# Token gathers of 128 rows in place of 96 or 64 in a mixture-of-experts layer

## The chip, the core and the metric

The kernel is one program on one core of a Trainium2 chip. The metric is the device time of one execution in microseconds. Engines are named as the profile names them: PE is TensorE (PEld its weight loads), DVE VectorE, ACT ScalarE, POOL GpSimd, SP SyncE. SP and POOL also issue DMAs, each on a queue of its own, and both queues are served by the core's 16 DMA engines.

## The reference

One decoder layer on 512 tokens of width 1024, all in float32: two kinds of attention with one output projection, a layer norm giving x1, then a mixture of experts and a second layer norm. The part that matters here is the experts:

```python
logits = xf @ w_router + b_router            # 512 tokens, 32 experts
top_vals, top_idx = lax.top_k(logits, 4)
gates = softmax(top_vals)
...
g = minimum(xb @ w_gate[e] + b_gate[e], 7)   # xb: the tokens of expert e
u = clip(xb @ w_up[e] + b_up[e], -7, 7)
h = g * sigmoid(1.702 * g) * (u + 1)
y_rows = h @ w_down[e] + b_down[e]
...
y = sum over k of gates[n, k] * y_rows[dest[n, k]]
```

Each expert has three matrices of 1024 x 1024 in float32, 12.58 MB, so the 32 experts hold 402.7 MB. With 2048 assignments an expert has 64 tokens on average.

## The kernel before

**Stages.** Attention, first layer norm and routing come first; x1 is written to `x1d` in DRAM, a row of 4 KiB for each token. Then the experts run one after the other, a step each (`Step`, lines 1103 to 1158; the loop is at line 1631). The experts are ordered by their number of tokens and dealt out to the steps alternately: the 16 fullest are *large* steps with 96 slots (64 and 32 more), the others *small* steps with 64 slots. From step 1 to step 29 large and small alternate: 15 large, 14 small. The last two experts, the emptiest, are routed as a pair. Tokens that find no slot would go through a loop behind the end (`overflow`), which has nothing to do for these inputs.

**A step.** `gate0`/`gate1`, `up` and `down` multiply the step's tokens with the three matrices. 64 slots are done with 64 columns of the array twice beside each other (`mat64`, line 624), a large step's other 32 slots with 32 columns four times (`mat32`, line 634, `matd32`, line 1046). The result, scaled by the gates, is added to `accd` in DRAM by one or two accumulating indirect DMAs on POOL's queue (`store`, line 1157): 128 rows of 2 KB (two per slot), and in a large step 128 rows of 1 KB.

**Weights.** `wload` (line 662) brings each matrix in two DMAs of 2 MB, 128 partitions of 16 KiB, issued by SP into a ring of eight tiles and one further tile (`wtile`, line 655). A tile is free again when PE has read it for the last time, and SP waits for that before it issues.

**Tokens of a step.** Two steps ahead, `do_route` makes the token numbers: a product with a one-hot matrix (`route_mm`, line 969) gives for each slot the number of its token in `ix`; an unfilled slot gets 0. The one-hot matrix has 128 columns: for 64 slots these are slots 0 to 63 twice, for the other 32 (the second column of `ix`) slots 64 to 95 four times. So `ix` has 128 rows, and those past the slots repeat slots of the same expert. `gather` (line 975) casts the numbers to integers in `ii` on DVE (lines 977, 979) and issues one indirect DMA on POOL (line 981) that reads those rows of `x1d` into the tile `xg`, slot by slot on the partitions. There is one `xg` buffer. `load_x` (line 1031) transposes the 64 or 96 rows on PE (line 1039) and ACT copies them out (line 1040).

**Other gathers.** Step 0's is written out on its own at line 864 (64 rows). That of the last two experts is at line 1027 (`route_pair`): 64 slots of each, 128 rows in one DMA. Step 1's goes through `route_tokens` and `gather`, steps 2 to 29 through `route` and `gather`.

Of the kernel before, what the change touches and what calls it, by code (L numbers as in the profile page):

```python
# [19 lines left out]
P = 128  # L20
# [82 lines left out]
def kernel(ctx: ExitStack, tc: tile.TileContext, a: dict, out: bass.AP, dbg=None):  # L103
    nc = tc.nc
    dbg = dbg or {}
    V, S, G, PE = nc.vector, nc.scalar, nc.gpsimd, nc.tensor
# [9 lines left out]
    x1d = dr.tile([T, D], F32, name="x1d")  # L116
# [856 lines left out]
                          start=(t == 0), stop=(t == NT - 1))  # L973

    def gather(n, ii, ix, large):
        Cn = 96 if large else 64
        V.tensor_copy(ii[0:64], ix[0:64, 0:1])  # L977
        if large:
            V.tensor_copy(ii[64:96], ix[64:96, 1:2])
        xg = p3.tile([P, D], F32, tag="xg", name=f"xg{n}")  # L980
        G.indirect_dma_start(out=xg[0:Cn], out_offset=None, in_=x1d,  # L981
                             in_offset=bass.IndirectOffsetOnAxis(ap=ii[0:Cn], axis=0))
        return xg

    def route_info(n, oh, rhs_t, large):
# [9 lines left out]
    def route_tokens(n, oh):  # L995
        px = bank(f"pxt{n}")
        route_mm(px, oh, lambda t: RT[:, t, 0:2, n], True, 0, 2)
        xs, ix, gt, ii = route_tiles(n)
        V.tensor_copy(xs[:, :, 0:2], px[:, 0:16].rearrange("p (a b) -> p a b", a=2)[:, :, 0:2])
        V.tensor_tensor(ix, xs[:, :, 0], xs[:, :, 1], ALU.add)  # L1000
        return xs, gather(n, ii, ix, True), ix, gt
# [8 lines left out]
    def route(n, oh, rhs_t, large):  # L1010
        ii, ix, gt = route_info(n, oh, rhs_t, large)
        return gather(n, ii, ix, large), ix, gt
# [700 lines left out]
```

## Time and profile before

| | us |
|---|---|
| median of 3 runs | 1354.06 |
| lowest, highest | 1352.81, 1355.06 |
| the profiled execution | 1354.38 |
| its span | 1352.6 |
| PE busy in the span | 1240.9 (92%) |
| DVE, ACT, POOL busy | 392.3, 262.7, 179.0 |
| queue q1 (SP's): packets, MB | 34848, 428.15 |
| queue q0 (POOL's): packets, MB | 10880, 24.78 |

The span runs from the first to the last instruction of the program; the execution takes 1.8 us more. PE's busy time is that of pipelined matmuls with modelled ends. The DMA share is the mean share of time in which the 16 DMA engines had a packet in work, from each packet's own duration, so it can exceed 1; the GB/s are the bytes of those packets.

### The profile page before, as it was taken

How to read it: one execution, taken by the hardware profiler on the slowest of the kernel's cores; microseconds unless marked ns; L12 is line 12 of the kernel's file. 1: busy time of each engine (PE TensorE's matmuls, PEld its weight loads, DVE VectorE, ACT ScalarE, POOL GpSimd, SP SyncE). 2: the span in 40 equal slices, each digit the busy share in tenths (PEclk: the TensorE clock that was granted, in tenths of full speed). 3: DMA queues.
4: the chain of work that ended last, by engine and by line, in shares of the span. 5: the costliest groups of instructions: out<-in, count | busy, mean ns of one | idle time of the engine just before them, and what ended most of it. 6: DMA issues, size and time to landing. Idle time of an engine off the chain costs nothing.

```text
span 1352.6 us, 20619 instructions
## 1 busy us (share of the span) xinstructions
PE 1240.9 (92%) x8596; PEld 577.6 (43%) x8596; DVE 392.3 (29%) x1020; ACT 262.7 (19%) x588; POOL 179.0 (13%) x184
## 2 busy tenths in 40 slices
PE   9999998898999999898989898989797989899985
PEld 8887555443344343333333333333333333333331
DVE  6765667453121211111111111111111111111125
ACT  5544655231101111011101010101010101010113
POOL 0540221001011011011010101010101010100013
PEclk9999999898999999999999999999999999899978
DMA  8031064489999999999999999999999999999992
GB/s 312 0 125 63 7 256 171 172 333 358 380 390 401 394 381 403 395 401 394 403 396 402 394 399 399 398 398 400 397 398 396 402 394 401 397 420 409 420 377 97
DMA packets 45824, 454.28 MB, mean 336 GB/s; under 512 B 5856, under 2 KB 8672, under 8 KB 20256
## 3 DMA queue, kind: packets, MB, share of 16 engines
q1 hardware_dynamic: 34848, 428.15, 78.3%
q0 software_dynamic: 10880, 24.78, 7.4%
q8 instruction: 69, 1.13, 0.3%
q14 instruction: 27, 0.22, 0.0%
HBM read 436.39 MB, written 16.52 MB: 335 GB/s over the span
## 4 chain that ended last, share of the span: by engine, by line
PE 57%; DMA 38%; DVE 2%; issue 1%; ACT 0%; SPq 0%; POOL 0%; POOLq 0%; DVEq 0%; ACTq 0%
DMA wu<-w_up 33%; PE pu L624 10%; PE pg L624 9%; PE pd L624 9%; PE puz L634 3%; PE mx L556 3%; DMA wd<-w_down 3%; PE pd L1046 2%; PE pj L200 2%; PE pj L201 2%; PE pj L202 2%; PE pxg L1039 1%; DMA xg<-x1d,ii 1%; PE sc L469 1%; PE av L510 1%; PE pgz L634 1%
## 5 line engine op out<-in xcount | busy, mean ns | idle before, releaser
L624 PE MATMUL pd<-wd,hT 128*64 128x512 f32 x1024 | 231.2, 602 | 14.1 <-DMA wd<-w_down 14.1
L1157 POOL DMA_INDIRECT accd<-y,si x46 | 73.5, 1598 | 534.4 <-ACT y L1162 356.6
L624 PEld LDWEIGHTS pd<-wd,hT 128*64 128x64 f32 x1024 | 73.5, 138 | 158.2 <-issue 138.6
L624 PE MATMUL pg<-wg,xgB 128*64 128x512 f32 x512 | 123.4, 626 | 17.2 <-DMA wg<-w_gate 17.2
L624 PE MATMUL pu<-wu,xgB 128*64 128x512 f32 x512 | 118.9, 618 | 0.0
L624 PE MATMUL pg<-wg,xgA 128*64 128x512 f32 x512 | 117.9, 600 | 0.0
L624 PE MATMUL pu<-wu,xgA 128*64 128x512 f32 x512 | 114.6, 596 | 1.8 <-DMA wu<-w_up 1.8
L1062 DVE TENSOR_SCALAR u<-pu 128x512 f32<-128x512 f32 x31 | 21.4, 691 | 324.6 <-PE pu L628 324.5
L634 PE MATMUL puz<-wu,xgB 128*32 128x256 f32 x960 | 70.7, 447 | 46.2 <-DMA wu<-w_up 46.2
L624 PEld LDWEIGHTS pg<-wg,xgB 128*64 128x64 f32 x512 | 38.6, 142 | 88.9 <-issue 87.0
L981 POOL DMA_INDIRECT xg<-x1d,ii x29 | 27.3, 941 | 350.5 <-DVE ii L977 232.7
L634 PEld LDWEIGHTS puz<-wu,xgB 128*32 128x32 f32 x960 | 34.2, 124 | 85.6 <-DMA wu<-w_up 38.3
L1040 ACT COPY xgB<-pxg 128x384 f32<-128x384 f32 (+1 forms) x32 | 14.6, 472 | 286.0 <-PE pxg L1039 285.9
L624 PEld LDWEIGHTS pu<-wu,xgB 128*64 128x64 f32 x512 | 36.5, 143 | 75.1 <-issue 74.5
L624 PEld LDWEIGHTS pu<-wu,xgA 128*64 128x64 f32 x512 | 34.9, 137 | 73.1 <-issue 66.9
L624 PEld LDWEIGHTS pg<-wg,xgA 128*64 128x64 f32 x512 | 34.8, 137 | 61.1 <-issue 59.5
L1062 DVE TENSOR_SCALAR uz<-puz 128x256 f32<-128x256 f32 x16 | 6.8, 424 | 185.5 <-PE puz L638 185.5
L1046 PE MATMUL pd<-wd,hT 128*32 128x256 f32 x1024 | 58.8, 381 | 0.0
L634 PE MATMUL pgz<-wg,xgB 128*32 128x256 f32 x960 | 57.1, 391 | 0.0
L1162 ACT ACTIVATE y<-pd,gt 128x512 f32<-128x512 f32 x30 | 20.6, 687 | 170.3 <-PE pd L624 170.3
L1052 DVE TENSOR_SCALAR g<-pg 128x512 f32<-128x512 f32 x32 | 22.1, 691 | 89.0 <-PE pg L628 89.0
L1040 ACT COPY xgA<-pxg 128x256 f32<-128x256 f32 x30 | 11.2, 372 | 189.2 <-PE pxg L1039 188.2
(447 smaller groups left out, 1517.3 us busy)
## 6 DMA issues: line engine op xcount, KB each, us to landing
wg<-w_gate SPq DMA_DIRECT2D x64, 2048.0 KB, 40.0
wu<-w_up SPq DMA_DIRECT2D x64, 2048.0 KB, 40.0
wd<-w_down SPq DMA_DIRECT2D x62, 2048.0 KB, 40.1
wd<-w_down SPq DMA_DIRECT2D x3, 1024.0 KB, 33.0
hat<-wB SPq DMA_DIRECT2D x1, 2048.0 KB, 12.8
hwk<-wB SPq DMA_DIRECT2D x1, 2048.0 KB, 17.0
hwv<-wB SPq DMA_DIRECT2D x1, 2048.0 KB, 7.2
hwk<-w_o SPq DMA_DIRECT2D x1, 2048.0 KB, 7.3
```

The lines of the kernel that those rows point to most:

```text
L200: PE.matmul(o, xh[:, k, tt], h[:, 0:n], start=(k == 0), stop=False)
L201: PE.matmul(o, xh[:, k, tt], l[:, 0:n], start=False, stop=False)
L202: PE.matmul(o, xl[:, k, tt], h[:, 0:n], start=False, stop=(k == KD - 1))
L556: PE.matmul(ps[h], attnT[:, k, t * P:(t + 1) * P], wo[k // 4][:, k % 4, hs], start=(k == 0), stop=(k == KD - 1))
L624: PE.matmul(ps[64 * c:64 * c + 64, :], xt[:, k, 0:64], w[k // 4][:, k % 4, hf * 512:(hf + 1) * 512], start=(st and k == 0), stop=(k == KD ...
L634: PE.matmul(o[32 * c:32 * c + 32, :], xt[:, k, 64:96], w[k // 4][:, k % 4, c * 256:(c + 1) * 256], start=(k == 0), stop=False)
L981: G.indirect_dma_start(out=xg[0:Cn], out_offset=None, in_=x1d, in_offset=bass.IndirectOffsetOnAxis(ap=ii[0:Cn], axis=0))
L1040: S.copy(xgT[:, 4 * h:4 * h + 4, 0:Cn], pt[:, :, 0:Cn])
L1046: PE.matmul(ps[32 * c:32 * c + 32, 0:256], ht[:, k, :], wd[k // 4][:, k % 4, c * 256:(c + 1) * 256], start=(k == 0), stop=(k == KD - 1))
L1052: V.tensor_scalar(g, pgt, 7.0, None, ALU.min)
L1062: V.tensor_scalar(u, pup, 7.0, -7.0, ALU.min, ALU.max)
L1157: G.indirect_dma_start(out=dst, out_offset=bass.IndirectOffsetOnAxis(ap=si[:, i:i + 1], axis=0), in_=self.y[:, lo:hi], in_offset=None, com ...
```

## The change

`gather` casts all 128 rows of the token numbers and gathers 128 rows in every step. For a small step rows 64 to 127 are the slots 0 to 63 again; for a large step rows 64 to 127 are the slots 64 to 95 twice. Nothing else is changed: `load_x` reads the rows that it read.

```diff
     def gather(n, ii, ix, large):
-        Cn = 96 if large else 64
-        V.tensor_copy(ii[0:64], ix[0:64, 0:1])
         if large:
-            V.tensor_copy(ii[64:96], ix[64:96, 1:2])
+            V.tensor_copy(ii[0:64], ix[0:64, 0:1])
+            V.tensor_copy(ii[64:P], ix[64:P, 1:2])
+        else:
+            V.tensor_copy(ii, ix[:, 0:1])
         xg = p3.tile([P, D], F32, tag="xg", name=f"xg{n}")
-        G.indirect_dma_start(out=xg[0:Cn], out_offset=None, in_=x1d,
-                             in_offset=bass.IndirectOffsetOnAxis(ap=ii[0:Cn], axis=0))
+        G.indirect_dma_start(out=xg, out_offset=None, in_=x1d,
+                             in_offset=bass.IndirectOffsetOnAxis(ap=ii, axis=0))
         return xg
```

## Rows read from the trace of the kernel before

**Rows 1.** The page, the span in 40 slices: DMA share in tenths, GB/s.

```profile
DMA  8031064489999999999999999999999999999992
GB/s 312 0 125 63 7 256 171 172 333 358 380 390 401 394 381 403 395 401 394 403 396 402 394 399 399 398 398 400 397 398 396 402 394 401 397 420 409 420 377 97
```

**Rows 2.** The page, the chain that ended last: by engine, by line.

```profile
PE 57%; DMA 38%; DVE 2%; issue 1%; ACT 0%; SPq 0%; POOL 0%; POOLq 0%; DVEq 0%; ACTq 0%
DMA wu<-w_up 33%; PE pu L624 10%; PE pg L624 9%; PE pd L624 9%; PE puz L634 3%; PE mx L556 3%; DMA wd<-w_down 3%; PE pd L1046 2%; PE pj L200 2%; PE pj L201 2%; PE pj L202 2%; PE pxg L1039 1%; DMA xg<-x1d,ii 1%; PE sc L469 1%; PE av L510 1%; PE pgz L634 1%
```

**Rows 3.** The chain in order of time: start us, us, what.

```profile
366.46 7.02 PE pu L624 x32
...
423.75 7.02 PE pu L624 x32
...
581.65 7.85 PE pu L624 x32
...
607.56 37.84 DMA wu<-w_up
...
648.80 7.02 PE pu L624 x32
```

**Rows 4.** Windows: from:to, length, busy us by engine, PE clock, DMA share, GB/s.

```profile
320.00:345.00 25.00, 20.49 (x198) 9.20 (x198) 3.77 (x11) 1.79 (x4) 2.52 (x2) 0.86 0.92 318
345.00:366.00 21.00, 21.00 (x156) 8.77 (x155) 4.42 (x13) 3.06 (x6) 2.52 (x2) 1.00 0.99 401
...
716.76:1300.00 583.24, 527.89 (x3760) 211.42 (x3762) 94.34 (x256) 56.74 (x112) 58.18 (x46) 0.96 1.02 401
```

**Rows 5.** Windows, POOL alone: weights (2), gathers of 64, 96, 128, scatters (2).

```profile
592.00:599.00 7.00, 0.94 (x1) 1.00 1.01 430
...
1196.00:1203.00 7.00, 1.42 (x2) 1.00 1.00 428
414.60:421.60 7.00, 0.43 (x1) 1.00 0.99 342
...
1133.50:1140.50 7.00, 0.34 (x1) 1.00 1.01 346
561.50:568.50 7.00, 0.00 (x0) 1.00 1.03 344
...
1165.50:1172.50 7.00, 0.00 (x0) 1.00 1.02 337
1204.50:1211.50 7.00, 0.85 (x1) 1.00 1.02 428
611.00:618.00 7.00, 0.00 (x0) 1.00 1.04 386
555.50:561.50 6.00, 0.94 (x1) 1.00 1.03 394
```

**Rows 6.** Tile xg, whole span, then 590:610, 620:645 and 1195:1215: duration ns, start, landing.

```profile
L981 POOL DMA_INDIRECT xg<-x1d,ii x29: 923/942/959, 292.3 to 1161.7; - x29
...
L981 POOL DMA_INDIRECT xg<-x1d,ii x1: 942/942/942, 596.3 to 596.3; - x1
...
DMA to landing us min/median/max: 9.7/9.7/9.7
...
L1039 PE MATMUL pxg<-cst,xg x8: 270/271/318, 621.2 to 622.1; 64*128 64x64 f32 x8
...
L1027 POOL DMA_INDIRECT xg<-x1d,ii x1: 1019/1019/1019, 1200.5 to 1200.5; - x1
...
DMA to landing us min/median/max: 10.8/10.8/10.8
```

**Rows 7.** Step 2's gather (landing, PE's wait) and casts in order of time.

```profile
DMA to landing us min/median/max: 9.0/9.0/9.0
...
324.94 1.11 PE L1039 MATMUL pxg<-cst,xg 64*128 64x64 f32 x8 [4.51 <-DMA xg<-x1d,ii]
...
595.39 0.15 DVE L977 CAST ii<-ix 64x1 int32<-64x1 f32 x1
```

## The prediction

> **What bounds the kernel now.** I read the page's slices first. From the tenth slice to the last but one the DMA digit is 9 and the GB/s line stays between 358 and 420 [rows 1]. The chain of work that ended last is shared between TensorE and DMA, and nearly all its DMA is one entry, the wait for the up weights (33% of the span) [rows 2]. In order of time the chain changes character. Early on a pair of experts (one large step, one small step) follows from TensorE alone: the up projection at 366.46 and the next at 423.75 are 57.3 us apart. Later the same pair takes 581.65 to 648.80, which is 67.2 us, and it has a weight transfer of 37.84 us in it [rows 3]. So TensorE could run a pair in 57.3 us and the weight stream needs 67. Before 345 us the stream sometimes has no free ring slot (318 GB/s, DMA share 0.92 in 320 to 345). From 345 us on the share is about 1 up to 1300 us [rows 4]. In that long stretch the time is the work of the DMA engines, and a transfer on the GpSimd queue costs what it takes from the weights beside it.
>
> The DMA share cannot price that: it counts the time packets took, and reads about 1 whether packets are fast or stretched. GB/s can. Rows 5 give it for short stretches. With weights alone the core moves 430, 433 and 428 GB/s (three stretches, the first and last shown), mean 430.3. Around a 64-row gather, seven stretches of 7 us lie between 328 and 349 GB/s, mean 340.1 (first and last shown). Around a 96-row gather, six lie between 337 and 347, mean 343.0 (first and last shown). Around the only gather on 128 rows, that of line 1027 for the last two experts, the stretch reads 428 GB/s, like weights alone [rows 5]. That is the observation on which the forecast rests: the short gathers take away far more than their own bytes, and the 128-row one does not.
>
> **Price of one gather.** The price is the stretch, less the time the weights moved in it would have taken alone: 7 us - (7 us x GB/s - own bytes) / 430.3. A row is 4 KiB.
> - 64 rows (262 KB): 7 - (2381 - 262)/430.3 = 2.08 us.
> - 96 rows (393 KB): 7 - (2401 - 393)/430.3 = 2.33 us.
> - 128 rows (524 KB): 7 - (2996 - 524)/430.3 = 1.26 us.
>
> The prices can be checked on a whole pair. Its weights, 2 x 12.58 MB at 430.3, take 58.5 us. Two scatters of 128 x 2 KB (386 GB/s in 7 us, 1.33 us each) and one of 128 x 1 KB (394 GB/s in 6 us, 0.81 us) make 3.5 us [rows 5]. With gathers of 2.08 and 2.33 us the sum is 66.4 us, against the 67.2 seen [rows 3]. At the 128-row gather's price per row the two short gathers would make only 1.6 us, and the sum would be 3.6 us short of what is seen, so their excess is real work of the stream and not a local blur.
>
> **The change part by part.**
> - *Gathers in the saturated stretch.* Line 981 issues 29 gathers, from 292.3 us on [rows 6]. Those of steps 1 to 3 come before 345 us. The other 26 are 13 of 64 rows and 13 of 96, since large and small steps alternate. If each then costs what the one at line 1027 costs, a small one saves 2.08 - 1.26 = 0.82 us and a large one 2.33 - 1.26 = 1.07 us: 13 x 0.82 + 13 x 1.07 = 24.6 us. For the new gather I take line 1027's price because it has the same form: 128 rows of 4 KiB from x1d into the same tile, through one index column, in the same stream. The other end is the price per row of the short gathers (rivals). A better price than 1.26 us is hardly possible, since 524 KB alone are 1.22 us at 430.3 GB/s.
> - *The three early gathers.* Up to 345 us the weight stream is held by ring slots that TensorE has yet to free, so a cheaper gather there is given back: nothing gained. One of them costs. Step 2's gather lands 9.0 us after issue and TensorE stands 4.51 us for it [rows 7]. The 64-row gather at 596.3 landed after 9.7 us, the 128-row one after 10.8 [rows 6]. TensorE thus waits 1.1 to 1.8 us longer, frees its slots later by as much, and the stream idles for it. I take +1.5 us, with bounds 0 and 1.8.
> - *Landing later elsewhere.* The gather at 596.3 landed by 606.0, and its first reader, the transposes of line 1039, starts at 621.2 [rows 6]. That is 15 us of cover for 1 to 2 us. If the cover were gone TensorE would stand for the difference once a step, at most 26 x 1.8 us, but TensorE has 67.2 - 57.3 = 10 us to spare in each pair.
> - *Issue on GpSimd.* 1.02 us against 0.94 a gather [rows 6], +0.08 us 29 times. What is queued behind is the scatter of the step's result, which waits for TensorE anyway: 0.
> - *Index casts.* A small step still has one cast, on 128 rows instead of 64; a large one still two, the second on 64 rows instead of 32. A cast of 64 x 1 takes 0.15 us [rows 7]; between nothing and as much again, 0.15 us per gather, which the 15 us of cover hide: 0.
> - *Unchanged.* The load into TensorE still reads only 96 or 64 rows of the tile (line 1039), so there is no more work behind it. Line 864's early gather and the pair's at 1027 are not touched. The rows added hold repeats that nobody reads.
>
> Sum: -24.6 + 1.5 = -23.1 us. The profiled execution took 1354.4 us (span 1352.6), so 1331.3. The median of the runs shown is 0.3 us below that execution. Forecast **1331 us**.
>
> [...]
>
> **Rivals.**
> 1. *Bytes only (slower).* Line 1027's gather is a single sample, and it may be cheap for its place, late in the stream, not for its 128 rows. Then added rows cost what its rows cost, 1.26/128 = 9.8 ns each: +0.63 us per small and +0.31 us per large gather, 13 x 0.94 = +12.3, with the early wait +13.8 us: **1368 us**. For it: one sample. Against it: weights alone move 428 GB/s just before it and 430 at 592 us [rows 5], so the stream is not easier there. [...]
> 2. *Price per row of the short gathers (slower).* If the cause is the gather's rows as such, a small one adds 64 x 2.08/64 = 2.08 us and a large one 32 x 2.33/96 = 0.78 us: 13 x 2.86 = +37, with the wait **1393 us**. Against it: line 1027 again, and that 96 rows cost only 1.12 times 64. The point from which it turns: a 128-row gather above 2.15 us, that is under 373 GB/s in its 7 us, makes the kernel slower.
> 3. *Half the gain.* The added rows read the same rows of x1d as slots of the other half, at about the same moment, and this may cost. Unfilled slots already all read token 0, at line 1027 too, and nothing shows there. **1343 us.**
> 4. *Nothing moves.* The stream gets faster and another bound takes over. TensorE's 57.3 us against some 65.3 for the new pair [rows 3] leaves no room for it; only a stream that runs dry after 345 us could do it. Within 0.2% (2.7 us, about what a measurement of this kernel can tell from no change): **1354 us**.
>
> **How the numbers follow.** Forecast 0.77, rival 3 0.08, rival 4 0.04, rival 1 0.07, rival 2 0.04. The forecast's own range is 1325 to 1338: the early wait at 0 and a GB/s reading off by 2 or 3 in each stretch on one side, 0.7 of the gain on the other. To 1345 it takes in rival 3, and 0.85 of the chance. Faster by over 0.2%: 0.77 + 0.08 = 0.85; same 0.04; slower 0.07 + 0.04 = 0.11.
>
> **What the changed profile would show.** Right: 7 us stretches around gathers after 345 us at about 425 GB/s instead of 340; pairs of about 65.3 us; bytes on the software queue up by 5.6 MB (1376 rows) and the span shorter all the same; TensorE's wait for step 2's gather near 6 us instead of 4.5. Wrong: gathers' stretches still near 340 to 370 GB/s (rivals 1 and 2), stretches at 425 but pairs still at 67 (rival 4), or stretches around 385 (rival 3). The forecast as a whole falls if line 1027's gather is cheap for another reason than its 128 rows.

## The result and the profile after

The changed kernel takes 1334.73 us (median of 4 runs, 1332.74 to 1337.12) against 1354.56 us for the kernel before on the same chip: a ratio of 0.9854 with a 95% interval of 0.9832 to 0.9876, or 19.8 us less. A second measurement beside other kernels (after_again, below) gives 1333.96 us and 0.9859 (0.9842 to 0.9875). One kernel below (half_quarter_late) has times in two groups 15 us apart, and its interval spans both.

The page of the kernel after: DMA share in tenths and GB/s of the 40 slices, POOL's queue (packets, MB, share), and the chain that ended last.

```profile
DMA  8031074579999999999999999999999999999992
GB/s 316 0 127 64 1 265 158 182 276 367 362 400 413 409 421 413 412 420 412 421 414 417 415 417 415 419 413 419 412 421 410 418 411 419 413 419 414 419 373 94
q0 software_dynamic: 12256, 30.41, 8.1%
PE 61%; DMA 35%; DVE 2%; ACT 0%; issue 0%; SPq 0%; POOL 0%; POOLq 0%; DVEq 0%; ACTq 0%
DMA wu<-w_up 29%; PE pu L624 11%; PE pg L624 10%; PE pd L624 10%; PE puz L634 4%; PE mx L556 3%; DMA wd<-w_down 3%; PE pd L1047 3%; PE pj L200 2%; PE pj L201 2%; PE pj L202 2%; DMA xg<-x1d,ii 2%; PE pgz L634 2%; PE pxg L1040 2%; PE av L510 1%; PE sc L469 1%
```

From the tenth slice on the DMA digits are the same as in [rows 1], but the bytes are not. Most slices after the twelfth stand between 410 and 421 GB/s, where most stood at 394 to 403. POOL's queue moves 5.63 MB more than before, and yet the kernel is shorter. In the chain the up weights fall from 33% [rows 2] to 29%.

The chain in order of time (start us, us, what), where [rows 3] had pairs of 67.2 us:

```profile
580.07 7.99 PE pu L624 x32
...
606.54 35.20 DMA wu<-w_up
...
643.83 7.02 PE pu L624 x32
...
669.33 38.35 DMA wu<-w_up
...
711.08 7.35 PE pu L624 x32
```

Two pairs take 580.07 to 711.08, that is 65.5 us each. The stream still decides: the chain still has a transfer of up weights of 35 to 38 us in each. TensorE works on other matrices during most of it; it stands idle for 47.5 of the 583.24 us from 716.76 on (busy 535.74, below).

Windows of the kernel after (from:to, length, POOL busy, PE clock, DMA share, GB/s): around three gathers of small steps, then three of large ones. They answer to [rows 5].

```profile
599.00:606.00 7.00, 0.80 (x1) 1.00 1.00 421
729.30:736.30 7.00, 0.73 (x1) 1.00 1.02 428
859.20:866.20 7.00, 0.68 (x1) 1.00 1.02 431
...
692.00:699.00 7.00, 0.00 (x0) 1.00 1.02 435
822.50:829.50 7.00, 0.00 (x0) 1.00 1.03 437
...
1083.50:1090.50 7.00, 0.00 (x0) 1.00 1.01 428
```

Six such stretches at small steps have a mean of 427.5 GB/s and six at large steps 429.8. The prediction's formula then gives 1.26 and 1.23 us per gather, so 1.25 us for any of them, where 64 rows cost 2.08 and 96 cost 2.33.

Two windows of the kernel after over long stretches (now with PE, PEld, DVE, ACT and POOL busy ahead of PE clock, DMA share and GB/s), beside [rows 4]:

```profile
320.00:345.00 25.00, 17.64 (x184) 8.10 (x182) 5.10 (x18) 1.79 (x4) 3.23 (x3) 0.80 0.80 293
...
716.76:1300.00 583.24, 535.74 (x3788) 215.24 (x3786) 102.04 (x272) 62.74 (x118) 58.53 (x46) 0.96 1.01 414
```

In the saturated stretch the core moves 414 GB/s instead of 401. In the early stretch it moves less than before, 293 instead of 318. This is where step 2's gather costs time, and it costs more than forecast. Below, in order of time (start us, us, engine, line, operation, and in brackets the idle time before it and its releaser): first the kernel before, then the kernel after.

```profile
301.83 0.66 PE L1088 MATMUL pht<-cst,u 128*128 128x128 f32 x4 [0.59 <-DVE u L1063]
...
351.29 0.60 PE L1088 MATMUL pht<-cst,u 128*128 128x128 f32 x4
```

```profile
303.81 0.66 PE L1089 MATMUL pht<-cst,u 128*128 128x128 f32 x4 [0.58 <-DVE u L1064]
...
317.79 0.96 POOL L982 DMA_INDIRECT xg<-x1d,ii  x1 [22.51 <-DVE si L1156]
...
329.77 1.11 PE L1040 MATMUL pxg<-cst,xg 64*128 64x64 f32 x8 [7.36 <-DMA xg<-x1d,ii]
...
356.47 0.60 PE L1089 MATMUL pht<-cst,u 128*128 128x128 f32 x4
```

TensorE stands idle for 7.36 us until step 2's gather has landed, where it was 4.51 us [rows 7]. In the chain after, the gather takes (start us, us from issue to landing):

```profile
317.79 11.85 DMA xg<-x1d,ii
```

The transposes of step 0's result and those of step 1's lie 52.66 us apart instead of 49.46. The 3.2 us are lost between them. The 2.0 us by which this execution is already late at step 0 come before the first changed gather is used, and the second profile (after_again) does not have them.

### The profile page after: what moved, and what is told of

Read it like the earlier page. It is cut to its first block, busy times and chain, and to the rows that moved or that the text cites. A ratio compares the mean times of both kernels' runs of the same rounds, so it can differ in the third digit from the quotient of the medians.

```text
span 1333.8 us, 20619 instructions
## 1 busy us (share of the span) xinstructions
PE 1233.7 (92%) x8596; PEld 575.8 (43%) x8596; DVE 391.4 (29%) x1020; ACT 262.7 (20%) x588; POOL 179.8 (13%) x184
## 3 DMA queue, kind: packets, MB, share of 16 engines
q0 software_dynamic: 12256, 30.41, 8.1%
## 4 chain that ended last, share of the span: by engine, by line
PE 61%; DMA 35%; DVE 2%; ACT 0%; issue 0%; SPq 0%; POOL 0%; POOLq 0%; DVEq 0%; ACTq 0%
DMA wu<-w_up 29%; PE pu L624 11%; PE pg L624 10%; PE pd L624 10%; PE puz L634 4%; PE mx L556 3%; DMA wd<-w_down 3%; PE pd L1047 3%; PE pj L200 2%; PE pj L201 2%; PE pj L202 2%; DMA xg<-x1d,ii 2%; PE pgz L634 2%; PE pxg L1040 2%; PE av L510 1%; PE sc L469 1%
## 5 line engine op out<-in xcount | busy, mean ns | idle before, releaser
L624 PE MATMUL pg<-wg,xgB 128*64 128x512 f32 x512 | 116.6, 597 | 4.0 <-DMA wg<-w_gate 4.0
L1054 ACT ACTIVATE sg<-g 128x512 f32<-128x512 f32 x32 | 20.1, 629 | 128.5 <-DVE g L1053 117.7
```

Of the source, the lines that this page charges most:

```text
L624: PE.matmul(ps[64 * c:64 * c + 64, :], xt[:, k, 0:64], w[k // 4][:, k % 4, hf * 512:(hf + 1) * 512], start=(st and k == 0), stop=(k == KD ...
```

## Experiments

The theory after the result: a gather whose rows lie on all 128 partitions costs the weight stream little more than its bytes (1.25 us, of which 524 KB at 430.3 GB/s are 1.22), and one on a part of them, whichever part and however many rows, holds up the weights that move beside it (2.08 and 2.33 us, of which the bytes are 0.61 and 0.91). Rivals were that only rows or bytes count (with line 1027 cheap for its place), that the repeats matter, and that the gain comes from one kind of step alone. All kernels below compute the whole layer.

| kernel | us | ratio to before (95%) | sum from the prices |
|---|---|---|---|
| small_only | 1347.32 | 0.9957 (0.9940 to 0.9973) | 1346.9 |
| large_only | 1338.74 | 0.9888 (0.9871 to 0.9904) | 1340.5 |
| two_64 | 1397.92 | 1.0325 (1.0304 to 1.0345) | 1393.3 |
| rows_112 | 1368.72 | 1.0111 (1.0094 to 1.0128) | 1366.9 |
| after_again | 1333.96 | 0.9859 (0.9842 to 0.9875) | 1332.9 |
| other_tokens | 1333.97 | 0.9854 (0.9836 to 0.9872) | 1332.9 |
| keep_early | 1331.94 | 0.9839 (0.9826 to 0.9853) | 1329.7 |
| half_rows | 1324.99 | 0.9799 (0.9779 to 0.9820) | 1322.9 |
| half_late | 1327.96 | 0.9799 (0.9785 to 0.9813) | 1322.3 |
| half_quarter_late | 1331.57 | 0.9813 (0.9770 to 0.9856) | see there |

The sums start at 1354.5 and exchange the prices of the 26 gathers behind 345 us (2.08, 2.33, 1.25, and those read below). They add 3.2 us for step 2 where its gather is one DMA of 112 or 128 whole rows. With half rows it is 0.6 us. In two_64, where step 2 reads only the first of its two DMAs, it is 0.7 us: TensorE waits 5.45 us there, and the two sets of transposes are 50.15 us apart.

**One kind of step alone** (small_only, large_only). In the first the condition is `not large`, in the second `large`; other steps keep the old code.

```diff
     def gather(n, ii, ix, large):
+        if not large:        # large_only: if large
             ... (the changed gather, 128 rows)
+            return xg
+        Cn = 96 if large else 64
+        ... (the gather before)
```

> The 14 small gathers have 128 rows, the 15 large ones their 96 as before. Theory (each gather has its own price: 2.08 us at 64 rows, 2.33 at 96, 1.26 to 1.31 at 128): 13 x 0.8 = 10.4 us less than before in the saturated stretch, and step 2's gather lands later, which cost 2.8 us in the changed kernel's trace: 1347 us. Rival (the gain comes from the large gathers alone, and small ones at best pay for their added bytes): 1354 or more.

> The 15 large gathers have 128 rows, the 14 small ones their 64. Theory: 13 x 1.05 = 13.7 us less than before, and no later landing at step 2: 1340.5 us. With the run on small steps alone the two gains add up to the whole change's, 20 us. Rival (the gain comes from the small ones): 1354.

The two came out at 1347.32 and 1338.74 us. Their ratios stand for 5.8 and 15.2 us less than before, 21.0 together, against 19.1 to 19.8 for the whole change. Both kinds contribute, and the small steps pay the early wait out of their gain. A small step's gather has twice the bytes it had and still gives time back, which is the opposite of what bytes alone would do.

**The same rows in two DMAs** (two_64).

```diff
-        G.indirect_dma_start(out=xg, out_offset=None, in_=x1d,
-                             in_offset=bass.IndirectOffsetOnAxis(ap=ii, axis=0))
+        jj = p3.tile([64, 1], I32, tag="jj", name=f"jj{n}", bufs=3)
+        V.tensor_copy(jj, ix[64:P, 1:2] if large else ix[0:64, 0:1])
+        for r, iv in ((slice(0, 64), ii[0:64]), (slice(64, P), jj)):
+            G.indirect_dma_start(out=xg[r], out_offset=None, in_=x1d,
+                                 in_offset=bass.IndirectOffsetOnAxis(ap=iv, axis=0))
```

> The same 128 rows as in the change, as two DMAs of 64 rows, one to partitions 0 to 63 and one to 64 to 127. Theory (a DMA that covers half of the partitions holds up the weights, whichever half and however many rows there are in all): each gather costs 2 x 2.08 = 4.2 us, so 2.1 more than before for a small and 1.8 for a large step, 13 x 3.9 = 51 us over before: about 1405. Rival (128 rows spread over all partitions are cheap together, in one DMA or two): as the change, 1335 to 1340.

It took 1397.92 us, some 63 us more than the change with the same rows, the same bytes and the same places. Windows of two_64 around two of its gathers, 10 us each:

```profile
617.00:627.00 10.00, 1.58 (x1) 1.00 1.01 324
...
1034.50:1044.50 10.00, 1.58 (x1) 1.00 1.02 315
```

Six of them have a mean of 324.7 GB/s, hence 10 - (3247 - 524)/430.3 = 3.67 us for the two DMAs, 1.84 each. Two DMAs of 64 rows on the two halves do not make a cheap whole, so neither the rows nor the bytes of a step set the price, but how they are cut into DMAs. That is somewhat under the 4.2 us expected. If the first costs 2.08 us as before, the second, on the other half, costs 1.59 us, and its 262 KB alone would take 0.61 us at 430.3 GB/s. In all these runs a DMA has as many rows as partitions, so 128 rows in one DMA and 128 partitions are not told apart.

**112 rows** (rows_112).

```diff
-        G.indirect_dma_start(out=xg, out_offset=None, in_=x1d,
-                             in_offset=bass.IndirectOffsetOnAxis(ap=ii, axis=0))
+        G.indirect_dma_start(out=xg[0:112], out_offset=None, in_=x1d,
+                             in_offset=bass.IndirectOffsetOnAxis(ap=ii[0:112], axis=0))
```

> Every gather has 112 rows. Theory (128 rows are a case of their own, and the price below goes up with the rows: 2.08 at 64, 2.33 at 96, so some 2.45 at 112): 13 x (0.37 + 0.12) = 6 us over before, 1360, plus up to 3 us at step 2. Rival (the price falls steadily as the gather fills the partitions, 2.33 at 96 to 1.31 at 128, so 1.8 at 112): 13 x (0.28 + 0.53) = 10.5 us less than before, 1344.

It took 1368.72 us. Windows of rows_112 around two gathers:

```profile
607.00:614.00 7.00, 0.57 (x1) 1.00 1.01 328
...
1013.00:1020.00 7.00, 0.76 (x1) 1.00 1.01 344
```

Six have a mean of 338.5 GB/s, which is 2.56 us a gather. The price goes 2.08, 2.33, 2.56 for 64, 96 and 112 rows and then 1.25 for 128. It does not fall as the partitions fill up; the last 16 rows halve it. The expected 1360 (and up to 3 us at step 2) was short by 6 us; 2.56 us in place of the 2.45 taken makes 26 x 0.11 = 2.9 us of them, and the rest is open.

**Other rows behind the slots** (other_tokens).

```diff
     def gather(n, ii, ix, large):
+        V.tensor_copy(ii[0:64], ix[0:64, 0:1])
         if large:
-            V.tensor_copy(ii[0:64], ix[0:64, 0:1])
-            V.tensor_copy(ii[64:P], ix[64:P, 1:2])
+            V.tensor_copy(ii[64:96], ix[64:96, 1:2])
+            V.tensor_copy(ii[96:P], C("tokid")[96:P, 0:1])
         else:
-            V.tensor_copy(ii, ix[:, 0:1])
+            V.tensor_copy(ii[64:P], C("tokid")[64:P, 0:1])
```

> The rows past the slots are not repeats: small steps fetch tokens 64 to 127 there, large ones tokens 96 to 127 (nobody reads these rows). Theory (it does not matter what is read): as the change, 1334.7. Rival (a repeated row is cheaper, or dearer, to read than another one): off by the share of the repeats, 0.1 us for each tenth of the price of 26 gathers, 3 us or more.

1333.97 us against 1333.96 for the change beside it. Which tokens the added rows read does not matter, so the cause that rival 3 of the prediction gave falls.

**The same tokens as half rows** (half_rows).

```diff
+    x1h = x1d.rearrange("t (h d) -> (t h) d", h=2)
...
+        if not large and n < E:
+            V.scalar_tensor_tensor(ii, ix[:, 0:1], 2.0, hfp, ALU.mult, ALU.add)   # 2 * token + half
+            G.indirect_dma_start(out=xg[:, 0:512], out_offset=None, in_=x1h,
+                                 in_offset=bass.IndirectOffsetOnAxis(ap=ii, axis=0))
...
+                for j in range(4):
+                    for c in range(2):
+                        r = slice(64 * c, 64 * c + 64)
+                        PE.matmul(pt[r, j, 0:64], xv[:, 4 * h + j, :], ident[:, r], start=True, stop=True)
```

> Small steps gather their 64 tokens as 128 half rows of 2 KiB (slot p on partition p its first half, on partition 64 + p its second), and sixteen products with the identity put them in place in the array in place of eight transposes; large steps as in the change. Theory (what makes a gather cheap is that it lies on all 128 partitions; then the price is that of its bytes): 0.66 us instead of 1.31 per small gather, 13 x 0.65 = 8.5 us less than the change, and step 2's gather lands some 2 us sooner: 1324 us. Rival (the price is per row moved, 128 of them): as the change, 1335.

> The changed kernel again, for comparison on the same chip with the runs beside it: 1334.7 us.

It took 1324.99 us beside 1333.96, 9.0 us less than the change and 28 less than before. Windows of half_rows around two gathers of small steps:

```profile
591.20:598.20 7.00, 0.81 (x1) 1.00 1.00 424
...
915.20:922.20 7.00, 0.68 (x1) 1.00 1.01 424
```

Six have a mean of 425.8 GB/s, 0.68 us a gather. The 64 tokens of a small step, 262 KB either way, cost 2.08 us as 64 rows on 64 partitions and 0.68 us as 128 half rows on 128. This is the clearest of the runs, because against the kernel before the bytes do not change. The packets do not change either. The DMA view of half_rows, POOL's queue (packets, MB, share):

```profile
q0 software_dynamic: 11360, 26.74, 7.4%
```

These are 896 packets fewer than after the change (12256), 64 for each of 14 small steps. So 128 half rows are moved in 64 packets of 4 KiB, as 64 whole rows are.

**The early gathers left as they were** (keep_early).

```diff
     def gather(n, ii, ix, large):
+        if n > 3:
             ... (the changed gather)
+            return xg
+        ... (the gather before)
```

> The gathers of steps 1 to 3 keep their 96 or 64 rows, all later ones have 128. Theory (step 2's 128-row gather makes TensorE wait 2.8 us longer before the weight stream is saturated, and this reaches the end): 1332 us, 2.8 below the change, and TensorE's wait for step 2's gather back at about 4.5 us. Rival (that delay is absorbed before the stream saturates, and the 2 us between forecast and result are of the price of a gather): as the change, 1334.7.

1331.94 us, 2.0 us below the change on the same chip. Its trace, in order of time:

```profile
301.45 0.66 PE L1098 MATMUL pht<-cst,u 128*128 128x128 f32 x4 [0.59 <-DVE u L1073]
...
324.79 1.11 PE L1049 MATMUL pxg<-cst,xg 64*128 64x64 f32 x8 [4.74 <-DMA xg<-x1d,ii]
...
350.89 0.60 PE L1098 MATMUL pht<-cst,u 128*128 128x128 f32 x4
```

The wait is back at 4.74 us and the two sets of transposes at 49.44 us apart. So step 2's wait is what 128 rows cost early, and the delay reaches the end, by 2 us of the 3.2. All five times (up to 1332.29 us) lie below all four of after_again (from 1332.65) on the same chip. The ratios (0.9839 and 0.9859, intervals that overlap) do not settle what became of the rest.

**Both together** (half_late): half rows and 128 rows from step 4 on, the old gathers in steps 1 to 3.

> The gathers of steps 1 to 3 and their transposes as before the change; from step 4 on small steps gather half rows, large ones 128 rows. Theory (the two gains do not touch each other: half rows gave 9 us from the change, the early gathers 2 us, of which half rows had taken hardly any, since step 2's half rows landed 9.2 us after issue and their products took 1.1 us longer): 1323 us, 2 below half rows everywhere. Rival (the later start of the half-row kernel is made up elsewhere): 1325.

Its ratio is that of half_rows, 0.9799, so nothing is gained. The premise of the 2 us was wrong. In half_rows TensorE waits 4.75 us for step 2 and spends 1.1 us more on its products, and the two sets of transposes are 50.05 us apart (302.27 and 352.32), 0.6 us more than before; there is hardly anything left to take. The sum of prices misses half_late by 5.7 us, more than any other kernel. Its profiled execution is 1.6 us later than that of half_rows at step 0 already (303.91 against 302.27); where the rest goes no run shows.

**Quarter rows for the large steps** (half_quarter_late, half_quarter_again): from step 4 on the first 64 slots of a large step come as 128 half rows too, and slots 64 to 95 as 128 quarter rows in a second DMA, placed by 32 further products a step. The part of the edit for the second DMA:

```diff
+            if large:
+                iq = p3.tile([P, 1], I32, tag="iq", name=f"iq{n}", bufs=3)
+                V.scalar_tensor_tensor(iq, ix[:, 1:2], 4.0, hfq, ALU.mult, ALU.add)
+                G.indirect_dma_start(out=xg[:, 512:768], out_offset=None, in_=x1q,
+                                     in_offset=bass.IndirectOffsetOnAxis(ap=iq, axis=0))
```

> As the run beside it, and from step 4 on large steps gather their first 64 slots as 128 half rows and the other 32 as 128 quarter rows of 1 KiB, in two DMAs, 393 KB in place of 524. Theory (price by bytes on a full set of partitions): 0.69 + 0.35 = 1.04 us in place of 1.31 per large gather, 13 x 0.27 = 3.5 us less: 1319.5 us. Rival (a second DMA has a price of its own, or short pieces do): no gain or a loss, 1323 or more.

> The kernel of half_quarter_late once more, for a second profile. Theory (the stream has become cheap enough that TensorE's own pace decides, and the 48 small products in place of 8 transposes in each large step are what it pays with): where the granted clock stays near full, pairs of about 64 us with TensorE waiting for weights and some 1323 us; where it is 0.95, TensorE never waits and the pair takes 64.8 us, some 1338 us. Rival (the second DMA of a large step costs the stream): its gather stretches read well under 420 GB/s in both.

Of half_quarter_late three times lie at 1322.2 to 1324.5 us and three at 1338.6 to 1339.0. The single run of half_quarter_again, the same kernel, took 1322.8 us (the kernel before beside it 1351.13), too little for a ratio. One window over 650 us (PE, PEld, DVE, ACT, POOL busy, PE clock, DMA share, GB/s): first half_quarter_late's execution of 1338.7 us, then half_quarter_again, then half_rows.

```profile
450.00:1100.00 650.00, 650.00 (x5508) 292.24 (x5506) 112.06 (x311) 66.70 (x130) 77.44 (x60) 0.95 1.01 410
```

```profile
450.00:1100.00 650.00, 650.00 (x5656) 292.39 (x5654) 116.70 (x321) 68.07 (x132) 79.28 (x61) 0.99 1.02 415
```

```profile
450.00:1100.00 650.00, 614.14 (x4755) 257.23 (x4751) 115.31 (x315) 66.70 (x131) 68.99 (x51) 0.98 1.02 415
```

TensorE is busy in all 650 us of both executions of the quarter-row kernel, and in 614 of half_rows. With 0.95 of the clock granted (the mean of the window) its pairs take 64.9 us, with 0.99 they take 62.8 (means of eleven pairs from 444 us on). One stretch around a large step's gather in each, first half_quarter_late, then half_quarter_again:

```profile
646.80:653.80 7.00, 0.00 (x0) 1.00 1.01 426
```

```profile
639.20:646.20 7.00, 0.00 (x0) 1.00 1.02 429
```

Such stretches keep 425 to 431 GB/s in both executions (five in one, six in the other), so the second DMA is not the cause. TensorE has become the bound, and the time hangs on the granted clock: 0.952 in each of the three long times, 0.972 to 0.975 in the three short ones. Where little of the clock is lost, the cheaper gathers still buy something: the median of the three short times is 1323.4 us, 4.6 below half_late on the same chip, against 3.5 expected. In the three long times they buy nothing. That TensorE waited for weights in the faster execution, as expected, is not seen. Why the clock differs between executions of one program stays open.

## Why the prediction was right, point by point

- **The bound** was read rightly. The stream decides before and after; only its rate changed, from 401 to 414 GB/s between 716.76 and 1300 us.
- **The price of a 128-row gather** was right: 1.26 us from one sample before, 1.25 us on twelve stretches after. Rival 1 held that line 1027's gather was cheap for its place; now all twelve that were read are cheap, wherever they stand between 420 and 1155 us.
- **The gain of 24.6 us** in the saturated stretch follows again from the prices: 13 x (2.08 - 1.25) + 13 x (2.33 - 1.25) = 24.8. The runs on one kind of step alone share it out as the prices say, within 2 us each.
- **The early wait** is the term that was mis-sized: +1.5 us, at most 1.8, was put for it, and it is 3.2 us in the trace. The mechanism was right, the TensorE wait at step 2 and then a stream without free slots: SP's longest wait for a slot that TensorE has yet to free (by `pgz`, line 634) is 15.7 us in place of 13.0, and the core moves 293 GB/s in place of 318 from 320 to 345 us. The size was taken from one landing late in the stream (10.8 us), and the gather lands 11.85 us after issue at step 2 (317.79 to 329.64). The other three traces with 128 whole rows there agree (12.07 in after_again, 11.72 in small_only, 12.26 in other_tokens). The 128 half rows of half_rows land after 9.24 us, like the 64 rows of keep_early (9.24), so here it is not the partitions that count. Why a gather of 128 rows lands later there than at line 1027 no run shows.
- **The rest** of the difference between -23.1 and -19.8 us, some 1.6 us, is not traced to a cause. Two measurements of the kernel after differ by 0.8 us (1334.73 and 1333.96), and its profiled execution started 2.0 us late. That of after_again, without the late start, took 1332.65 us, 21.7 below the profiled execution before, and -24.8 + 3.2 = -21.6 us accounts for that.
- **The range's lower end**, 1325, lies below what its reasons give. Without the early wait the sum is 1329.8 us, and a reading off by 3 GB/s before and after is 0.05 us for each of 26 gathers both times, 2.5 us in all, hence 1327.
- **Edits put at zero** were zero as far as the trace shows: 0.99 us of issue on GpSimd in place of 0.94, later ends of the gathers behind 345 us (from issue to the last packet a median of 10.1 us in place of 8.4 at small steps, 12.5 in place of 10.9 at large ones) with no wait of TensorE for one, 5.63 MB more on POOL's queue.
- **Rivals.** Rival 1 (bytes, 1368) and rival 2 (price per row, 1393) fall by the result, and small_only, two_64 and half_rows say why. Rival 3 falls by other_tokens, rival 4 by the pairs of 65.5 us. The stretches stand at 417 to 438 GB/s, far above the 373 below which the kernel would have become slower.

Why a part of the partitions costs so much is not settled. The runs show that it goes by the single DMA, cheap with 128 rows on 128 partitions (1.25 us, against 3.67 for two of 64 rows), and that 112 of 128 do not help (2.56 us). The single packets in the traces show what is held up, in the windows read above. A weight packet of 16 KiB takes 612 ns on average with weights alone. Where its time overlaps that of a gather's packets it takes 824 ns beside the gathers of 64 rows and 770 beside 96 (the kernel before), 772 beside 112 (rows_112) and 826 beside the two of 64 (two_64). Beside 128 rows (the kernel after) it takes 617 ns at small and 612 at large steps, and 619 beside half rows (half_rows). So the short gathers slow the weights' own packets, and the full ones leave them as they are. By what mechanism a shorter gather does so no run here shows: the traces give a packet's queue, start, duration and size, but not which of the 16 DMA engines moved it.

## What to carry to other kernels

Where the DMA engines are saturated, price a small transfer by the GB/s of the stretch around it, less its own bytes, and not by its bytes, its landing or the DMA share, which reads about 1 at 337 as at 430 GB/s [rows 5]. Look whether a gather covers all 128 partitions: padding it with rows that nobody reads was worth 1.5% here, and cutting half of the gathers into pieces that fill the partitions, without a byte more, brought this to 2.0%. Then look at the first gathers, before the stream is saturated, where latency counts and a longer gather costs (here 11.85 us to landing in place of 9.0, and 3.2 us of time); and at what becomes the bound next: with the large steps' gathers cut into pieces too, it was TensorE, busy in all 650 us of the window.

## What the hardware showed that was not expected

The price of one gather beside a saturated stream rises from 2.08 us at 64 rows to 2.33 at 96 and 2.56 at 112, and drops to 1.25 us at 128. It is 0.68 us for 64 tokens as 128 half rows. Two gathers of 64 rows one behind the other cost 3.67 us, nearly three times one of 128. The weights' own packets show the same: 770 to 826 ns beside the short gathers, 612 to 619 ns beside those on all partitions, and 612 alone.
